# Norm vectors and q's and k's first weight blocks loaded from ScalarE's queue, x^T's first two blocks at the head of SP's

## The chip, the cores and the metric

The kernel runs on one core of one Trainium2 chip. The metric is device time in microseconds (us): the median of three runs before the change is 1878.91 us (1877.92 to 1880.84). All data is float32. Engines: PE is TensorE (matmuls; its weight loads are shown as PEld), ACT is ScalarE, DVE is VectorE, POOL is GpSimd, SP is SyncE, which here only issues transfers.

## What is computed

One encoder layer on 512 tokens of width 2048. Only its beginning matters here: the norm, the projection by w_in, and of that the columns of head 0's q and k.

```python
h = rms_norm(x, pre_mix_g[l])
z = h @ w_in[l]                       # (512 x 2048) @ (2048 x 4096)
q = z[..., :ATTN_WIDTH]; k = z[..., ATTN_WIDTH:2 * ATTN_WIDTH]   # 8 heads of 128
v, u = ...
a = chunked_attention(q, k, v, rel_bias[l])
p = multiscale_pool(u, pool_w[l], pool_scale[l])
x = x + rms_norm(concat(a, p) @ w_o[l], post_mix_g[l])
# then a gated feed-forward of width 5632 with a causal depthwise convolution
```

## The kernel before

**Precision.** A float32 product is made of three matmuls of a reduced format: each operand is split into a high part (ACT rounds it: lines 143 and 146) and a low part (DVE takes what is left: lines 144 and 147), and `mm3` (lines 159 to 161) multiplies high by high, then with one low part, then with the other. Line 146 and 147 also multiply by the norm's gain, which is a column of the tile `vec`. The token's own norm factor is applied later, so the first products need only x^T, the gains and the weights.

**The first loop.** The inner dimension of 2048 is cut into 16 blocks of 128 rows, kb = 0 to 15. For each kb the kernel loads block kb of x^T (128 x 512, 256 KB, into the tiles `xT0` to `xT3`, four blocks in each), splits it into `hT`, and adds 2 x 3 matmuls of 512 columns, three for q and three for k of head 0, to two accumulators. q's and k's weights come in pieces of 1, 3, 4, 4 and 4 blocks (`chunks`), each piece one transfer for q and one for k: 64 KB each for kb = 0, 192 KB each for kb = 1 to 3, 256 KB each for four blocks. Their rows are 128 elements, that is 512 bytes; a row of x^T is 2 KB.

**What sets the order.** PE's order is the order of the program. On the other engines a scheduler orders the instructions at build time; SP keeps the loop's order of transfers. In it SP issues `vec` (line 122, 28 KB), then block 0 of x^T (line 266), q's and k's first pieces (line 271), block 1 of x^T, q's and k's pieces for kb = 1 to 3, then blocks 2, 3 and 4 of x^T, the pieces for kb = 4 to 7, and so on. ACT and DVE take the splits about in this order and each split waits for its own transfer. Transfers signal on eight semaphores in turn, so that from the ninth on the issuing queue waits until the transfer eight places earlier has landed.

**Before the first product.** ACT loads its table (line 130) and does a small activation. PE does nine matmuls of zeros (line 136, 18 passes) from 1.09 us on, while the first transfers are under way.

**Behind the loop.** The loop is followed by v's products and the rest of the layer. v's weights, and all others, come through rings of buffers that are loaded ahead on SP's and POOL's queues.

Of the kernel before, what the change touches and what calls it, by code (L numbers as in the profile page):

```python
# [15 lines left out]
P = 128  # L16
# [7 lines left out]
ATTN = HEADS * DH  # L24
# [19 lines left out]
V_CONV = V_PSCALE + 8  # L44
# [7 lines left out]
def rows(w, r0, c0, a, b):  # L52

    return w[r0:r0 + a * P, c0:c0 + b].rearrange("(a p) c -> p a c", p=P)
# [23 lines left out]
def encoder_layer(ctx: ExitStack, tc: tile.TileContext, x, xT, vecs, rel, post_mix, post_ffn,  # L78
# [7 lines left out]
    nc = tc.nc  # L86
# [18 lines left out]
    def bank(name, at=None):  # L105
        if at is None:
            at = cycle.pop(0)
            cycle.append(at)
        pool = psum if at < 2 else upper_pool
        return pool.tile([P, 512], F32, tag=f"ps{at}", bufs=1, name=name)  # L110

    def acc8(name, which, dt=F32):
        return acc.tile([P, 2048], dt, tag="acc" + which, bufs=2, name=name)

    def raw4(name):
        return big.tile([P, 1024], F32, tag="raw", bufs=6, name=name)

    def w4(name):
        return big.tile([P, 1024], F32R, tag="w4", bufs=8, name=name)

    vec = const.tile([P, V_ALL], F32, name="vec")
    nc.sync.dma_start(vec[:, :V_CONV], vecs[:, :V_CONV])
    ident = const.tile([P, P], F32, name="ident")
    make_identity(nc, ident)
    ones = const.tile([P, 1], F32, name="ones")
# [12 lines left out]
    def col(v, i):  # L138
        return vec[:, v + i:v + i + 1]

    def split(hi, lo, src, scale=None):
        if scale is None:
            rounded = nc.scalar.activation(hi, src, AF.Copy)  # L143
            split.low = nc.vector.tensor_sub(lo, src, f32(hi)).ins  # L144
        else:
            rounded = nc.scalar.activation(hi, src, AF.Copy, scale=scale)
            nc.vector.scalar_tensor_tensor(lo, src, scale, f32(hi), op0=ALU.mult, op1=ALU.subtract)
        split.last = rounded.ins
        return rounded.ins
# [8 lines left out]
    def mm3(ps, l, r, first, last):  # L158
        nc.tensor.matmul(ps, l[0], r[0], start=first, stop=False)  # L159
        nc.tensor.matmul(ps, l[0], r[1], start=False, stop=False)  # L160
        nc.tensor.matmul(ps, l[1], r[0], start=False, stop=last)  # L161
# [4 lines left out]
    def hT4(name, shape):  # L166
        return whole(name).rearrange("p (s a b) -> p s a b", s=2, a=shape)
# [4 lines left out]
    def blk(hT, kb, sl=slice(None)):  # L172
        return tuple(hT[kb // 4][:, part, kb % 4, sl] for part in range(2))
# [20 lines left out]
    def halves(name, w, c0, a, b):  # L194
        n = KD // a
        return [(f"{name}_{i}", rows(w, i * a * P, c0, a, b), a, b) for i in range(n)]

    def head_cols(what, h):
        return {"q": 0, "k": ATTN, "u": 3 * ATTN}[what] + h * P

    def qk_specs(h):
        return halves(f"q{h}", w_in, head_cols("q", h), 8, P), halves(f"k{h}", w_in, head_cols("k", h), 8, P)
# [8 lines left out]
    for h in range(1, HEADS):  # L211
        q, k = qk_specs(h)
# [14 lines left out]
    for n in WO_ORDER:  # L227
        for cc in range(2):
            s = [(f"wo{n}{cc}_{q}", rows(wo_factor[n], q * 256, cc * S, 2, S), 2, S) for q in range(4)]
# [24 lines left out]
    R = const.tile([P, S], F32, name="R")  # L254
    rt = const.tile([P, NT], F32, name="rt")
    const.tile([P, 40], F32, name="place")
    xt = [acc8(f"xT{i}", "AABB"[i]).rearrange("p (a b) -> p a b", a=4) for i in range(4)]
    hT = [hT4(f"hT{i}", 4) for i in range(4)]
    first = {}
    for s in [s for pair in zip(*qk_specs(0)) for s in pair]:  # L260
        first[s[0]] = raw4(s[0] + "r"), w4(s[0] + "h"), w4(s[0] + "l")
    ps0 = {what: bank(what + "0") for what in "qk"}
    chunks = {0: 1, 1: 3, 4: 4, 8: 4, 12: 4}
    for kb in range(KD):
        i, o = divmod(kb, 8)
        nc.sync.dma_start(xt[kb // 4][:, kb % 4, :], xT[kb * P:(kb + 1) * P, :])
        for what in "qk":
            if kb in chunks:
                raw, hi, lo = first[f"{what}0_{i}"]
                sl = slice(o * P, (o + chunks[kb]) * P)  # L270
                nc.sync.dma_start(raw[:, sl].rearrange("p (a b) -> p a b", b=P),
                                  rows(w_in, kb * P, head_cols(what, 0), chunks[kb], P))
                split(hi[:, sl], lo[:, sl], raw[:, sl])
        last_split = split(*blk(hT, kb), xt[kb // 4][:, kb % 4, :], col(V_PREMIX, kb))
        for what in "qk":
            _, hi, lo = first[f"{what}0_{i}"]
            sl = slice(o * P, (o + 1) * P)
            mm3(ps0[what], (hi[:, sl], lo[:, sl]), blk(hT, kb), kb == 0, kb == KD - 1)
# [464 lines left out]
    def hold_rows(tag, name):  # L743
        return [hold(tag, f"{name}{i}", F32).rearrange("p a b -> p (a b)") for i in range(2)]
# [252 lines left out]
    with tc.tile_pool(name="p2", bufs=1, reuse_waits="tile") as p2:  # L997
# [51 lines left out]
        def load_x(t):  # L1049
            xs = hold_rows("wl", f"x{t}")  # L1050
            for j in range(2):
                nc.sync.dma_start(xs[j], x[(2 * t + j) * P:(2 * t + j + 1) * P, :])
            return xs
# [539 lines left out]
```

## Time and profile before

| | |
|---|---|
| median of three runs | 1878.91 us (1877.92 to 1880.84) |
| profiled execution: time, span | 1880.33 us, 1878.6 us |
| outside the span | 1.73 us |
| PE busy | 1859.6 us, 99% of the span |
| DVE, ACT, POOL busy | 80%, 51%, 16% |
| chain that ended last | PE 95%, DVE 2%, ACT 1%, DMA 1%, issue 1% |
| PE idle in the first 50 us | 3.05 us of 50 |
| mean granted clock of PE | 0.997 |

The span runs from the first to the last instruction; the execution's own time is 1.73 us longer. Busy time of PE includes the matmuls of zeros at the start. The granted clock is given as a share of full speed (2.4 GHz); 0.5 is 1.2 GHz. An "xcount" in a row of a timeline or a window counts instructions.

### The profile page before, as it was taken

The page shows a single profiled execution, that of the slowest core. Times are in us where ns is not written, and L with a number is a line of the kernel's source. Part 1 is how long each engine was busy: PE and PEld are TensorE (multiplying, and loading weights), DVE is VectorE, ACT ScalarE, POOL GpSimd, SP SyncE. Part 2 cuts the span into 40 slices and gives each one's busy share as a digit, 9 for nine tenths or more (in the row PEclk, how much of TensorE's full clock was granted, in tenths as well). Part 3 has the DMA queues.
Part 4 walks back from the last instruction along what each step waited for, and adds up shares of the span by engine and source line. Part 5 has one row for each costly group of instructions (what it writes and reads, how often), then busy time and mean ns, then how long its engine had stood idle before and what let it go on. Part 6 is the DMA issues. An engine that isn't in the chain of part 4 may idle for free.

```text
span 1878.6 us, 25181 instructions
## 1 busy us (share of the span) xinstructions
PE 1859.6 (99%) x9674; PEld 1596.4 (85%) x9674; DVE 1499.5 (80%) x1824; ACT 953.6 (51%) x1172; POOL 296.0 (16%) x387
## 2 busy tenths in 40 slices
PE   9999999999999999999999999999999899999998
PEld 7888888888889988888888888888888788888886
DVE  5445445587588989888888888888889899999877
ACT  6333233346488555555455554555545655565543
POOL 4101000000001111221221111111110112222221
PEclk9999999999999999999999999999999999999999
DMA  9747856676877778797977767667677799999997
GB/s 334 214 112 169 228 148 171 166 186 216 286 284 213 213 192 213 187 213 184 230 184 189 183 157 192 165 179 184 156 176 247 223 277 251 252 239 233 222 227 238
DMA packets 177913, 391.41 MB, mean 208 GB/s; under 512 B 11264, under 2 KB 62848, under 8 KB 174720
## 3 DMA queue, kind: packets, MB, share of 16 engines
q1 hardware_dynamic: 130720, 250.32, 40.4%
q0 software_dynamic: 47072, 139.48, 38.5%
q8 instruction: 76, 1.25, 0.3%
q14 instruction: 45, 0.37, 0.1%
HBM read 333.13 MB, written 98.57 MB: 230 GB/s over the span
## 4 chain that ended last, share of the span: by engine, by line
PE 95%; DVE 2%; ACT 1%; DMA 1%; issue 1%; SPq 0%; POOL 0%; POOLq 0%; DVEq 0%; ACTq 0%
PE q L978 27%; PE q L984 14%; PE p L160 6%; PE p L161 6%; PE p L159 6%; PE q L160 3%; PE q L161 3%; PE q L159 3%; PE m L160 2%; PE m L161 2%; PE m L159 2%; PE u L159 2%; PE v L159 2%; PE u L160 2%; PE v L161 2%; PE u L161 2%
## 5 line engine op out<-in xcount | busy, mean ns | idle before, releaser
L978 PE MATMUL q<-gT,wfh 128*128 128x512 f32 x1264 | 329.5, 392 | 0.0
L978 PEld LDWEIGHTS q<-gT,wfh 128*128 128x128 f32 x1264 | 233.1, 189 | 40.6
L978 PE MATMUL q<-h,wfh 128*128 128x512 f32 x960 | 253.7, 392 | 0.1
L143 ACT ACTIVATE wfh<-wx 128x1024 fp32r<-128x1024 f32 x167 | 174.9, 1059 | 131.8 <-PE q L984 72.5
L144 DVE TENSOR_TENSOR wfl<-wx,wfh 128x1024 fp32r<-128x1024 f32 x167 | 202.2, 1221 | 37.3 <-ACT wfh L143 37.2
L160 PE MATMUL p<-bl,ah 128*128 128x512 f32 x544 | 212.6, 391 | 1.8 <-DVE bl L144 1.8
L159 PE MATMUL p<-bh,ah 128*128 128x512 f32 x544 | 212.3, 390 | 1.9 <-ACT bh L143 1.6
L161 PE MATMUL p<-bh,al 128*128 128x512 f32 x544 | 212.3, 390 | 1.8 <-DVE al L144 1.8
L978 PEld LDWEIGHTS q<-h,wfh 128*128 128x128 f32 x960 | 178.3, 189 | 31.1 <-issue 0.4
L984 PEld LDWEIGHTS q<-gT,wfl 128*128 128x128 f32 x1264 | 172.4, 190 | 12.3
L984 PE MATMUL q<-gT,wfl 128*128 128x256 f32 x1264 | 176.2, 282 | 0.0
L143 ACT ACTIVATE bh<-b 128x2048 fp32r<-128x2048 f32 x68 | 129.8, 1917 | 86.7 <-DVE b L687 65.7
L144 DVE TENSOR_TENSOR bl<-b,bh 128x2048 fp32r<-128x2048 f32 x68 | 154.7, 2287 | 10.9 <-PE p L160 6.0
L815 POOL DMA_DIRECT2D wx<-in_w_up x86 | 75.8, 882 | 539.7 <-DVE wfl L144 430.9
L984 PEld LDWEIGHTS q<-h,wfl 128*128 128x128 f32 x960 | 131.0, 190 | 9.4
L984 PE MATMUL q<-h,wfl 128*128 128x256 f32 x960 | 133.9, 282 | 0.0
L143 ACT ACTIVATE wfh<-wy 128x1024 fp32r<-128x1024 f32 x82 | 87.1, 1062 | 86.3 <-PE q L984 81.5
L159 PEld LDWEIGHTS p<-bh,ah 128*128 128x128 f32 x544 | 102.5, 188 | 24.2 <-ACT bh L143 2.0
L160 PEld LDWEIGHTS p<-bl,ah 128*128 128x128 f32 x544 | 102.5, 188 | 23.4 <-DVE bl L144 2.1
L161 PEld LDWEIGHTS p<-bh,al 128*128 128x128 f32 x544 | 102.5, 188 | 23.3 <-DVE al L144 2.2
L730 POOL DMA_DIRECT2D sum<-part x60 | 72.0, 1238 | 256.5 <-DVE part L721 112.9
L144 DVE TENSOR_TENSOR wfl<-wy,wfh 128x1024 fp32r<-128x1024 f32 x82 | 99.8, 1217 | 2.3 <-ACT wfh L143 2.3
(454 smaller groups left out, 3823.6 us busy)
## 6 DMA issues: line engine op xcount, KB each, us to landing
wx<-in_w_up POOLq DMA_DIRECT2D x86, 512.0 KB, 8.0
b<-in_w_down SPq DMA_DIRECT2D x39, 1024.0 KB, 9.0
sum<-part POOLq DMA_DIRECT2D x70, 512.0 KB, 9.3
wx<-in_w_up SPq DMA_DIRECT2D x45, 512.0 KB, 3.6
wy<-in_w_up SPq DMA_DIRECT2D x44, 512.0 KB, 4.6
wz<-in_w_up SPq DMA_DIRECT2D x44, 512.0 KB, 6.1
wy<-in_w_up POOLq DMA_DIRECT2D x39, 512.0 KB, 6.7
wo_sum<-in_w_o POOLq DMA_DIRECT2D x16, 1024.0 KB, 12.0
```

What stands on the lines that cost most here:

```text
L143: rounded = nc.scalar.activation(hi, src, AF.Copy)
L144: split.low = nc.vector.tensor_sub(lo, src, f32(hi)).ins
L159: nc.tensor.matmul(ps, l[0], r[0], start=first, stop=False)
L160: nc.tensor.matmul(ps, l[0], r[1], start=False, stop=False)
L161: nc.tensor.matmul(ps, l[1], r[0], start=False, stop=last)
L730: nc.gpsimd.dma_start(dest, v, accum_op=ALU.add)
L815: self.last_add = nc.gpsimd.dma_start(self.raw[k, what], self.block(k, m, kh), accum_op=ALU.add).ins
L978: nc.tensor.matmul(ps.rearrange("p (a b) -> p a b", a=2), w[0][:, kb], both(h_f[i], kb), start=kb == 0, stop=kb == 7)
L984: nc.tensor.matmul(ps[:, :T], w[1][:, kb], at(h_f[i], kb)[0], start=False, stop=False)
```

## The change

`vec` and the two 64 KB pieces of q and k for kb = 0 are issued on ScalarE's queue instead of SP's. SP's queue begins with blocks 0 and 1 of x^T and then the 192 KB pieces for kb = 1 to 3; from block 2 of x^T on its order is the old one. The transfers of kb = 0 and 1 are issued ahead of the other setup (identity, constants, zeros for PE), the tiles for them are made there, and the loop leaves out what has been issued. No transfer changes its size, and no arithmetic changes.

```diff
-    nc.sync.dma_start(vec[:, :V_CONV], vecs[:, :V_CONV])
+    nc.scalar.dma_start(vec[:, :V_CONV], vecs[:, :V_CONV])
+    xt = [acc8(f"xT{i}", "AABB"[i]).rearrange("p (a b) -> p a b", a=4) for i in range(4)]
+
+    def load_x(kb):
+        nc.sync.dma_start(xt[kb // 4][:, kb % 4, :], xT[kb * P:(kb + 1) * P, :])
+
+    first = {}
+    for n in range(2):
+        for what in "qk":
+            first[f"{what}0_{n}"] = raw4(f"{what}0_{n}r"), w4(f"{what}0_{n}h"), w4(f"{what}0_{n}l")
+
+    def load_first(queue, what, kb, n):
+        queue.dma_start(first[f"{what}0_{kb // 8}"][0][:, kb % 8 * P:(kb % 8 + n) * P].rearrange("p (a b) -> p a b", b=P),
+                        w_in[kb * P:(kb + n) * P, (0 if what == "q" else ATTN):(0 if what == "q" else ATTN) + P].rearrange(
+                            "(a p) b -> p a b", p=P))
+
+    for what in "qk":
+        load_first(nc.scalar, what, 0, 1)
+    for kb in range(2):
+        load_x(kb)
+    for what in "qk":
+        load_first(nc.sync, what, 1, 3)
...
     for kb in range(KD):
         i, o = divmod(kb, 8)
-        nc.sync.dma_start(xt[kb // 4][:, kb % 4, :], xT[kb * P:(kb + 1) * P, :])
+        if kb > 1:
+            load_x(kb)
         for what in "qk":
             if kb in chunks:
                 raw, hi, lo = first[f"{what}0_{i}"]
                 sl = slice(o * P, (o + chunks[kb]) * P)
-                nc.sync.dma_start(raw[:, sl].rearrange("p (a b) -> p a b", b=P),
-                                  rows(w_in, kb * P, head_cols(what, 0), chunks[kb], P))
+                if kb > 1:
+                    load_first(nc.sync, what, kb, chunks[kb])
                 split(hi[:, sl], lo[:, sl], raw[:, sl])
```

SP's queue from the start of the program, before the change (names are tiles with a number behind them; xT0 holds blocks 0 to 3 of x^T, q0_0r and k0_0r the weights of kb = 0 to 7; DMAHW0 to 7 are the eight semaphores):

```order
L122 DMA vec_74<-in_vecs 128x56
L266 DMA xT0_106<-in_xT 128x512
L271 DMA q0_0r_114<-in_w_in 128x128
L271 DMA k0_0r_117<-in_w_in 128x128
L266 DMA xT0_106<-in_xT 128x512
L271 DMA q0_0r_114<-in_w_in 128x3x128
L271 DMA k0_0r_117<-in_w_in 128x3x128
L266 DMA xT0_106<-in_xT 128x512
L266 DMA xT0_106<-in_xT 128x512 [waits DMAHW0_49]
L266 DMA xT1_107<-in_xT 128x512 [waits DMAHW1_49]
L271 DMA q0_0r_114<-in_w_in 128x4x128 [waits DMAHW2_49]
```

SP's queue from the start, now (lines 126 and 134 are the two new helpers):

```order
L126 DMA xT0_76<-in_xT 128x512 x2
L134 DMA q0_0r_80<-in_w_in 128x3x128
L134 DMA k0_0r_83<-in_w_in 128x3x128
L126 DMA xT0_76<-in_xT 128x512
L126 DMA xT0_76<-in_xT 128x512 [waits DMAHW0_49]
L126 DMA xT1_77<-in_xT 128x512 [waits DMAHW1_49]
L134 DMA q0_0r_80<-in_w_in 128x4x128 [waits DMAHW2_49]
```

Block 2 of x^T, the third of line 126's, stands behind four transfers where it stood behind seven.

ACT from the start of the program, before the change (line 146 splits a block of x^T, line 143 a piece of weights):

```order
L130 ACT_TABLE_LOAD
L130 ACTIVATE table_85<-ones_81 128x1 [waits DVE_49]
L146 ACTIVATE hT0_110<-xT0_106,vec_74 128x512 [waits DMAHW1_49,DMAHW0_49]
L143 ACTIVATE q0_0h_115<-q0_0r_114 128x128 [waits DMAHW2_49]
L143 ACTIVATE k0_0h_118<-k0_0r_117 128x128 [waits DMAHW3_49]
L146 ACTIVATE hT0_110<-xT0_106,vec_74 128x512 [waits DMAHW4_49]
L143 ACTIVATE q0_0h_115<-q0_0r_114 128x384 [waits DMAHW5_49]
L143 ACTIVATE k0_0h_118<-k0_0r_117 128x384 [waits DMAHW6_49]
L146 ACTIVATE hT0_110<-xT0_106,vec_74 128x512 [waits DMAHW7_49]
```

ACT from the start, now (lines 167 and 164 are the old 146 and 143):

```order
L122 DMA vec_74<-in_vecs 128x56
L134 DMA q0_0r_80<-in_w_in 128x128
L134 DMA k0_0r_83<-in_w_in 128x128
L151 ACT_TABLE_LOAD
L151 ACTIVATE table_107<-ones_103 128x1 [waits DVE_49]
L164 ACTIVATE q0_0h_81<-q0_0r_80 128x128 [waits DMAHW2_49]
L167 ACTIVATE hT0_128<-xT0_76,vec_74 128x512 [waits DMAHW1_49,DMAHW0_49]
L164 ACTIVATE k0_0h_84<-k0_0r_83 128x128 [waits DMAHW4_49]
L164 ACTIVATE q0_0h_81<-q0_0r_80 128x384 [waits DMAHW5_49]
L167 ACTIVATE hT0_128<-xT0_76,vec_74 128x512 [waits DMAHW3_49]
L164 ACTIVATE k0_0h_84<-k0_0r_83 128x384 [waits DMAHW6_49]
L167 ACTIVATE hT0_128<-xT0_76,vec_74 128x512 [waits DMAHW7_49]
```

Three transfers stand ahead of the table load, and q's pieces for kb = 0 and for kb = 1 to 3 are now split ahead of block 0 and block 1 of x^T. DVE's order follows ACT's. PE's order is unchanged; further on, one pair of ACT's instructions (a square of x^T and the split of a piece of v's weights) changes places.

## Rows read from the trace of the kernel before

**Rows 1.** The page, part 1: busy us, share of the span, instructions.
```profile
PE 1859.6 (99%) x9674; PEld 1596.4 (85%) x9674; DVE 1499.5 (80%) x1824; ACT 953.6 (51%) x1172; POOL 296.0 (16%) x387
```

**Rows 2.** Waits of PE, whole run: us in total, times, longest.
```profile
PE q L159 <- ACT hT L146: 1.4, 1, 1.4
...
PE q L160 <- DVE hT L147: 0.3, 1, 0.3
```

**Rows 3.** Timeline of PE, first 16 us: start, us, operation [idle before it <- releaser].
```profile
1.09 4.21 PE L136 MATMUL idle<-early 128*128 128x128 f32 x18 [1.09 <-DVE early L128]
4.95 0.66 PE L159 MATMUL q<-hT,q_0h 128*128 128x512 f32 x1
...
8.99 0.50 PE L161 MATMUL k<-hT,k_0l 128*128 128x512 f32 x1
10.94 0.50 PE L159 MATMUL q<-hT,q_0h 128*128 128x512 f32 x1 [1.44 <-ACT hT L146]
11.72 0.50 PE L160 MATMUL q<-hT,q_0h 128*128 128x512 f32 x1 [0.28 <-DVE hT L147]
```

**Rows 4.** Windows: stretch, length; busy us of PE, PEld, DVE, ACT, POOL; PEclk, DMA, GB/s.
```profile
9.50:10.94 1.44, 0.00 (x1) 0.01 (x1) 0.02 (x1) 0.78 (x2) 0.00 (x0) 1.00 1.14 357
...
12.06:15.71 3.65, 3.65 (x11) 2.83 (x10) 3.57 (x7) 3.44 (x7) 0.00 (x0) 0.53 1.09 381
15.71:20.00 4.29, 4.29 (x20) 3.57 (x19) 4.25 (x8) 4.16 (x7) 0.00 (x0) 1.00 1.09 385
...
50.00:300.00 250.00, 250.00 (x1182) 210.15 (x1181) 119.80 (x216) 84.02 (x149) 16.65 (x41) 1.00 0.67 171
```

**Rows 5.** Timeline of ACT, first 25 us.
```profile
0.74 1.28 ACT L130 ACT_TABLE_LOAD   x1 [0.74 <-PEq L1582]
2.04 0.20 ACT L130 ACTIVATE table<-ones 128x1 f32<-128x1 f32 x1
3.91 0.72 ACT L146 ACTIVATE hT<-xT,vec 128x512 fp32r<-128x512 f32 x1 [1.67 <-DMA xT<-in_xT]
4.54 0.29 ACT L143 ACTIVATE q_0h<-q_0r 128x128 fp32r<-128x128 f32 x1
...
6.58 0.51 ACT L143 ACTIVATE q_0h<-q_0r 128x384 fp32r<-128x384 f32 x1
7.82 0.52 ACT L143 ACTIVATE k_0h<-k_0r 128x384 fp32r<-128x384 f32 x1 [0.74 <-DMA k_0r<-in_w_in]
10.16 1.98 ACT L146 ACTIVATE hT<-xT,vec 128x512 fp32r<-128x512 f32 x3 [1.82 <-DMA xT<-in_xT]
```

**Rows 6.** Timeline of SP's queue, first 25 us: start, us of issuing, transfer.
```profile
0.74 0.39 SPq L122 DMA_DIRECT2D vec<-in_vecs  x1
...
4.09 1.44 SPq L266 DMA_DIRECT2D xT<-in_xT  x3
```

**Rows 7.** DMA issues at 0.74, 3.56 and 4.09 us: KB each, us from issue to landing.
```profile
vec<-in_vecs SPq DMA_DIRECT2D x1, 28.0 KB, 1.9
...
k_0r<-in_w_in SPq DMA_DIRECT2D x1, 192.0 KB, 4.2
...
xT<-in_xT SPq DMA_DIRECT2D x1, 256.0 KB, 6.0
```

**Rows 8.** Windows of 1 us, columns as in Rows 4.
```profile
2.00:3.00 1.00, 1.00 (x7) 1.00 (x7) 0.00 (x0) 0.23 (x2) 0.47 (x15) 1.00 0.79 205
...
4.00:5.00 1.00, 1.00 (x8) 1.00 (x6) 0.33 (x1) 0.83 (x2) 0.00 (x0) 1.00 0.63 199
...
7.00:8.00 1.00, 0.86 (x3) 0.39 (x3) 0.93 (x2) 0.26 (x2) 0.00 (x0) 1.00 0.73 184
...
9.00:10.00 1.00, 0.49 (x2) 0.17 (x1) 0.00 (x0) 0.00 (x0) 0.00 (x0) 1.00 1.04 361
```

**Rows 9.** The page, part 5, POOL's issues: busy us, mean ns of one, idle before.
```profile
L815 POOL DMA_DIRECT2D wx<-in_w_up x86 | 75.8, 882 | 539.7 <-DVE wfl L144 430.9
...
L730 POOL DMA_DIRECT2D sum<-part x60 | 72.0, 1238 | 256.5 <-DVE part L721 112.9
```

More of the change, by code (lines that the diff above doesn't have):

```diff
@@ L256, in encoder_layer @@
     const.tile([P, 40], F32, name="place")
-    xt = [acc8(f"xT{i}", "AABB"[i]).rearrange("p (a b) -> p a b", a=4) for i in range(4)]
     hT = [hT4(f"hT{i}", 4) for i in range(4)]
-    first = {}
-    for s in [s for pair in zip(*qk_specs(0)) for s in pair]:
-        first[s[0]] = raw4(s[0] + "r"), w4(s[0] + "h"), w4(s[0] + "l")
     ps0 = {what: bank(what + "0") for what in "qk"}
```

## The prediction, made before the changed kernel ran

> **What bounds the kernel now.** I read the engines' shares first, then PE's waits, then the first 20 us engine by engine, since the change touches nothing else. PE is busy for 99% of the span [rows 1], so a change can gain only what PE loses, and it must lie where PE waits. Of PE's waits the loop that the change touches has two worth naming, 1.4 us and 0.3 us [rows 2]. Both stand at the same place: the last matmul of kb = 1 starts at 8.99 and ends at 9.49, the first of kb = 2 starts at 10.94, the second, which needs the low part of the same block, at 11.72 [rows 3]. The reader is to follow this back: ACT splits block 2 of x^T from 10.16, after 1.82 us without work, and is released by a transfer [rows 5]; that transfer was issued at 4.09 [rows 6] and took 6.0 us to land [rows 7], that is until 10.1. So **the landing of block 2 of x^T** sets when PE goes on, and from there on it is not stopped again in this loop: it is busy for 4.29 of 4.29 us at 15.71 to 20, and for 250 of 250 at 50 to 300 [rows 4].
>
> The gap has a second price. PE's granted clock is 1.00 in the gap, and from 12.06 to 15.71 its mean is 0.53, so nearly all of that at the lower of the two levels (1.2 GHz, against 2.4) [rows 4]. Over 3.65 us that is 0.47 x 3.65 = 1.7 us of lost matmul time. Everything that a change to this start could give back is thus some 1.4 + 0.3 + 1.7 = 3.4 us, under 0.2% of the time (3.8 us), about what a measurement of this kernel can tell from no change. That bounds the whole matter before any detail, but for a start of PE ahead of 4.95, which the zeros of line 136 exclude: they run from 1.09 to 5.30, and the first real matmul overlaps their end [rows 3].
>
> **Part 1, SP's queue is shorter.** Before block 2 of x^T SP issues seven transfers, from 0.74 to 4.09 [rows 6], so 3.35 / 7 = 0.48 us each. Now it issues four: block 2 goes out at 0.74 + 4 x 0.48 = 2.66, 1.43 us earlier. The semaphores that the next ones wait for are those of the vectors, block 0 of x^T and so on; the vectors landed 1.9 us after their issue [rows 7], that is by 2.7 if issued at 0.74 on ACT, so SP isn't held at block 3.
>
> How much of the 1.43 us reaches the landing depends on what filled the 6.0 us. The vectors needed 1.9 us with little else in flight, the 192 KB for k 4.2, block 2 of x^T 6.0 [rows 7]: the longer the queue, the later the landing, so a good part of it is waiting in the 16 DMA engines, and the same bytes stand ahead of block 2 after the change as before. If the engines had been full all the time, the landing would move by nothing; if never, by 1.43. They had pauses: their share was 0.79 in 2 to 3 us, 0.63 in 4 to 5 and 0.73 in 7 to 8, against 1.04 in 9 to 10, when transfers stood in line [rows 8]. Taken against 1.04 these three slices hold 0.25 + 0.41 + 0.31 = 0.97 us of pause ahead of block 2's landing, and an issue that is 1.43 us ahead can fill them. I take **1.0 us**, with 0 and 1.43 as bounds; it lies nearest to the rows of the engines' share, since they count the thing itself. The landing comes at 9.1, and the first matmul of kb = 2 at 10.94 - 1.0 = 9.9.
>
> **Part 2, ACT issues three transfers first.** No row shows a transfer issued by ACT. The nearest are SP's, 0.39 us (0.48 with the step to the next) [rows 6], and POOL's, 0.88 to 1.24 us [rows 9]. I take SP's 0.48, because both issue the same kind of load here and POOL's is another queue. ACT's table load then starts at 0.74 + 3 x 0.48 = 2.2, ends with its small activation 1.28 + 0.20 later, at 3.7, and the splits of q's piece (0.29) and of block 0 (0.72) end at 4.7 [rows 5], ahead of 4.95. Before, ACT stood idle for 1.67 us there [rows 5]; that idle time hides the issues. Cost nothing. At POOL's dearest price the table activation ends at 0.74 + 3.72 + 1.48 = 5.9 and the first real matmul would be near 7.0, two us late; but ACT would still have done kb = 1's splits (k's small piece 0.29 like q's, then 0.51, 0.72 and 0.52 [rows 5]: 2.0 us) by 9.0, before block 2 lands. PE would then finish kb = 1 about 10.3 instead of 9.9, which takes 0.4 us off the gain. So this part costs 0 to 0.4 us, and I take 0. Who waits behind the issues is the table load and all of ACT's splits; the cover is the gap before kb = 2.
>
> **Part 3, the new order on ACT and DVE.** Block 1 of x^T is now split behind q's 192 KB piece. Before, that piece was split at 6.58, in 0.51 us and with no idle time ahead of it [rows 5], so it had landed by then; if it lands no sooner now, block 1's split (0.72) runs from 7.1 to 7.8, just when k's piece is split in the trace, and kb = 1 ends as before, at 9.5. With the piece issued 1.43 us earlier it ends earlier. Either way kb = 2's block decides. Cost 0. q's and k's first pieces on their own queue share the engines with blocks 0 and 1; kb = 0 has its slack from the zeros, and all these bytes stand ahead of block 2 anyhow.
>
> **Part 4, the gap and the clock.** kb = 1's last matmuls wait for k's 192 KB piece, which ACT splits at 7.82 when it lands [rows 5]; this is issued 1.43 us earlier too and stands in the same line, so PE ends kb = 1 about 1 us earlier as well, at 8.5. The gap stays about 1.4 us, and after such a gap the clock fell in the trace. So I let the clock fall again for as long: no difference.
>
> **The sum.** 1.0 us of gain, 0 of cost: 1880.33 - 1.0 = 1879.3 for an execution like the profiled one (1878.6 span and 1.73 around it, which nothing here changes). The profiled execution lay 1.42 us above the median of the runs, so the median becomes 1878.91 - 1.0 = **1877.9 us**. The bounds of the terms alone (0 to 1.43, less up to 0.4) give 1877.5 to 1879.3.
>
> **Rivals.**
> *The clock holds (B).* If PE's gap becomes shorter, or falls at another moment, the clock may stay at 2.4 GHz, and 1.7 us more come back: 1878.91 - 2.7 = 1876.2. For it: the clock was still at 1.00 through the gap itself and fell only about when PE was back at full work [rows 4], so where the low stretch lies isn't fixed by the gap alone. Against it: the gap is likely to stay as long as it is. With the full 1.43 us and no gap at all it would be 3.4 us, or 1875.5.
>
> *The engines were the bound (D).* If the pauses in the share come from the 512-byte rows of the weights and not from late issues, no transfer lands sooner and the time stays at 1878.9. For it: in 7 to 8 us the share was 0.73 although block 2 had been issued three us before [rows 6, 8]; that pause wasn't SP's. Leaving that slice out, the gain of part 1 is 0.66 us, inside my range. The same result comes if a later stage, bound by its loads, takes the gain back. The Trainium skill (DMA: Bandwidth & Descriptors, section "Issuing engines are not separate DMA queues") speaks against the change here: transfers from several issuing engines share the same 16 DMA engines, and a second issuer saves only issue time, usually small beside the transfer. By that rule alone D would be the result.
>
> *The line gets deeper (C), slower.* Blocks 2, 3 and 4 of x^T were split without a break, 1.98 us for three [rows 5], so blocks 3 and 4 had landed nearly with block 2: the engines work on several transfers at once. Now q's and k's 256 KB for kb = 4 to 7 are also issued earlier, and if they are served among block 2's packets, each takes 256 KB at 357 GB/s [rows 4] = 0.73 us. With both, 1.46 - 1.0 = 0.5 us slower: 1879.4. It decides when more than 1.0 / 0.73 = 1.4 such transfers come in ahead that didn't before. Against it: they wait for the landing of earlier ones, and one queue serves in order.
>
> **How the numbers follow.** My forecast (A, 1877.9) 0.45; B 0.20; D 0.20; C 0.15. The range has to hold A to D: B's 1876.2 and C's 1879.4, each with about 0.9 us for the spread of a median whose three runs lay 2.9 us apart: 1875.2 to 1880.3. Faster by over 0.2% (below 1875.15) needs B, the full 1.43 us and a favourable draw: 0.06. Slower by over 0.2% (above 1882.7) isn't reached by any case; C with a dear issue on ACT, a second fall of the clock and an unfavourable draw: 0.04. Within 0.2%: 0.90.
>
> **What would show it.** In the new profile block 2 of x^T is issued near 2.7 and ACT splits it near 9.1; the first matmul of kb = 2 stands near 9.9, that of kb = 0 still near 4.9; ACT's three issues take 1.4 us in all and its table load starts near 2.2; the clock has one low stretch of some 3.6 us. I am wrong if block 2 still lands at 10.1 (D) or later (C), if the low stretch is gone (B) or comes twice, or if ACT's issues take 1 us each and the first product starts at 6 or later.

## The result

The changed kernel takes **1889.06 us** (median of five runs, 1888.38 to 1890.05) against 1878.91 (five runs, 1877.56 to 1880.84): ratio 1.0057, 95% interval 1.0046 to 1.0068. It is slower by 10 us, where 1.0 us of gain was forecast and the range ended at 1880.3. The profiled execution took 1889.9 us, its span is 1888.1.

The start of the program, on which the prediction spent all its working, is faster in this profile than in the profile before. The loss is 1.45 ms later.

### The profile page after: what moved, and what is told of

It is laid out like the page before. It is cut to its first block, busy times and chain, and to the rows that moved or that the text cites. A ratio compares the mean times of both kernels' runs of the same rounds, so it can differ in the third digit from the quotient of the medians.

```text
span 1888.1 us, 25181 instructions
## 1 busy us (share of the span) xinstructions
PE 1859.9 (99%) x9674; PEld 1597.7 (85%) x9674; DVE 1499.5 (79%) x1824; ACT 952.6 (50%) x1172; POOL 296.0 (16%) x387
## 4 chain that ended last, share of the span: by engine, by line
PE 96%; DVE 2%; DMA 1%; ACT 1%; issue 0%; POOL 0%; SPq 0%; POOLq 0%; ACTq 0%; DVEq 0%
PE q L996 27%; PE q L1002 14%; PE p L180 7%; PE p L182 7%; PE p L181 7%; PE q L181 3%; PE q L180 3%; PE q L182 3%; PE m L181 2%; PE m L182 2%; PE m L180 2%; PE k L180 2%; PE k L182 2%; PE k L181 2%; PE u L180 2%; PE v L180 2%
## 5 line engine op out<-in xcount | busy, mean ns | idle before, releaser
L180 PE MATMUL p<-bh,ah 128*128 128x512 f32 x544 | 213.0, 392 | 13.4 <-ACT bh L164 13.4
```

## The profile after

Waits of PE over the whole run, after the change (as [rows 2]: us in total, times, longest; the lines have moved, 180 to 182 are the old 159 to 161, 164 the old 143):

```profile
PE p L180 <- ACT bh L164: 13.4, 1, 13.4
PE p L181 <- DVE bl L165: 1.5, 1, 1.5
...
PE q L180 <- ACT hT L167: 0.7, 1, 0.7
```

The 1.4 us of [rows 2], ahead of kb = 2, is gone; at the start there is now a wait of 0.7 us ahead of kb = 0. And one single wait of 13.4 us stands in another stage: `p` are the products of the last stage (the feed-forward's output with w_down), `bh` the high part of a piece of w_down.

The start, timeline of PE (as [rows 3]):

```profile
1.09 4.21 PE L157 MATMUL idle<-early 128*128 128x128 f32 x18 [1.09 <-DVE early L149]
6.03 0.80 PE L180 MATMUL q<-hT,q_0h 128*128 128x512 f32 x1 [0.72 <-ACT hT L167]
...
11.21 0.39 PE L180 MATMUL q<-hT,q_0h 128*128 128x512 f32 x1
...
13.93 0.39 PE L180 MATMUL q<-hT,q_0h 128*128 128x512 f32 x1
```

These are the first products of kb = 0, 2 and 4. kb = 0 starts 1.1 us later than in [rows 3], kb = 2 with no pause ahead of it, and kb = 4 at 13.93, where the kernel before has it at 15.94: 2.0 us are won by then. The timeline of ACT and SP's queue show why kb = 0 is late and kb = 2 isn't (as [rows 5] and [rows 6]):

```profile
0.74 0.41 ACTq L122 DMA_DIRECT2D vec<-in_vecs  x1
...
1.17 0.46 ACTq L134 DMA_DIRECT2D q_0r<-in_w_in  x1
...
2.15 1.28 ACT L151 ACT_TABLE_LOAD   x1 [2.15 <-issue]
2.66 2.12 SPq L126 DMA_DIRECT2D xT<-in_xT  x3
...
5.05 0.31 ACT L164 ACTIVATE q_0h<-q_0r 128x128 fp32r<-128x128 f32 x1 [1.41 <-DMA q_0r<-in_w_in]
...
7.52 1.93 ACT L167 ACTIVATE hT<-xT,vec 128x512 fp32r<-128x512 f32 x3
```

Landing times of these transfers (as [rows 7]: KB, us from issue to landing):

```profile
vec<-in_vecs ACTq DMA_DIRECT2D x1, 28.0 KB, 3.2
...
q_0r<-in_w_in ACTq DMA_DIRECT2D x1, 64.0 KB, 3.9
...
xT<-in_xT SPq DMA_DIRECT2D x1, 256.0 KB, 4.3
```

Block 2 of x^T is issued at 2.66 and lands 4.3 us later, at 7.0 instead of 10.1; ACT takes it up without waiting. q's first piece, issued at 1.17, needs 3.9 us and lands at about 5.05, and ACT, which splits it ahead of block 0, waits 1.41 us for it.

**Where the 13.4 us are.** SP's queue around 1440 us, first before the change, then after (start, us of issuing with the waits inside a group, transfer; `gc` are two halves of the gated product read back from HBM, `b` pieces and sums of w_down):

```profile
1434.31 3.70 SPq L623 DMA_DIRECT2D b<-in_w_down  x2
1438.45 0.92 SPq L623 DMA_DIRECT2D gc<-gd  x2
1439.42 3.80 SPq L623 DMA_DIRECT2D b<-wd_sum  x3
```

```profile
1432.29 3.71 SPq L641 DMA_DIRECT2D b<-in_w_down  x2
1436.11 21.10 SPq L641 DMA_DIRECT2D gc<-gd  x2
1457.26 2.58 SPq L641 DMA_DIRECT2D b<-wd_sum  x3
```

PE gets here 2.0 us earlier, and so does SP. But the two loads of gc take 21.10 us to go out instead of 0.92: the second is held. The wait table of SP's queue in 1430 to 1480 us of the changed kernel names the releaser. The second line is that of the same table of the kernel before, where PE holds SP for 2.4 us only:

```profile
SPq L641 <- PE p L182: 20.1, 1, 20.1
...
SPq L623 <- PE p L161: 2.4, 1, 2.4
```

SP waits for PE, and PE then waits for SP. The chain that ended last, after the change (start, us, what):

```profile
1457.26 0.68 SPq L641
1457.94 0.04 issue
1457.99 10.52 DMA b<-wd_sum
1468.51 0.02 issue
1468.53 1.92 ACT bh L164
```

and PE's first product behind it, after the change and before:

```profile
1470.49 0.80 PE L180 MATMUL p<-bh,ah 128*128 128x512 f32 x1 [13.42 <-ACT bh L164]
...
1460.64 0.49 PE L159 MATMUL p<-bh,ah 128*128 128x512 f32 x1 [1.57 <-ACT bh L143]
```

The second half of gc goes out at 1456.9, when PE comes to the end of the products it has (the last of them ends at 1457.07). Behind it go the three loads of `b`, which had gone out by 1443.2 before; then 10.52 us for the transfer, 1.92 for the split, and PE resumes. Before the change the same pause was 1.57 us (1459.07 to 1460.64). So PE comes 2.0 us earlier, loses 13.42 - 1.57 = 11.85 us and resumes 9.85 us late. The span is 9.5 us longer, since all that follows takes 0.35 us less: the later waits of this stage are shorter by 1.3 us (1.5 and 1.1 instead of 1.8, 1.8 and 0.3), and most of that is lost again behind the longer pause, where the products start 0.43 us apart up to 1478.10 (granted clock 0.50, the lower level, from 1470.49 to 1475); before the change they did so only up to 1466.12.

**Why the load of gc waits for PE.** The order of instructions on SP is the same there in both kernels. Its waits are not. Before:

```text
L623 DMA gc0_13133<-gd0_0_3583 128x2048 [waits DMAHW6_49,PE_49]
L623 DMA gc1_13135<-gd0_1_3584 128x2048 [waits DMAHW7_49,DMASW3_49]
L623 DMA b7_13138<-wd_sum7_3611 128x2048 [waits PE_49]
```

After:

```text
L641 DMA gc0_13133<-gd0_0_3583 128x2048 [waits DMAHW6_49,DMASW1_49]
L641 DMA gc1_13135<-gd0_1_3584 128x2048 [waits DMASW3_49,DMAHW7_49,DVE_49,PE_49]
L641 DMA b7_13138<-wd_sum7_3611 128x2048
```

`gc1` now waits for PE, `gc0` no longer. Here a load waits for PE when its buffer lies where an operand lay that PE still reads. So the places have moved, and the diff shows by what: it makes q's and k's first tiles (`raw4`, `w4`) at the top of the program, ahead of `hT`. All three kinds live in one pool, `big`, which lays its kinds out in the order in which they are first asked for. From the code's sizes, in KB per partition: before hT 0 to 64, raw 64 to 88, split weights 88 to 120; after raw 0 to 24, split weights 24 to 56, hT 56 to 120. The last stage lays its buffers over the freed pool from the bottom, `wh` at 0 to 16, then gc's two of 8 KB at 16 to 32. Before, both fell on an hT tile; now the second falls on two split weight tiles, one of which at that time holds the high part of a left factor of the stage's first products. No row of a profile prints an address, but the addresses in the two built programs agree with these places, and the count of PE's instructions that `gc1` waits for (7872) is that of the last product that reads this left factor. The same programs show one thing more: `b5`, the load after `b7`, waits for PE in both, but now for a later product (count 7873 instead of 7801); it lies on the low part of the same left factor. The experiments test whether the places make the loss.

## The experiments

The theory (P, place): the loss comes from the order in which tiles are first allocated, not from the loads. The first rival (T): the earlier transfers, or the semaphores in which they take turns, make the wait. Within the start three more things were open: what the issue time is worth, what the clock costs, and whether all three transfers had to move.

### Places put back, loads as changed

```diff
+    hT = [big.tile([P, 8 * S], F32R, tag="hT", bufs=4, name=f"hT{i}").rearrange("p (s a b) -> p s a b", s=2, a=4)
+          for i in range(4)]
     first = {}
...
-    hT = [hT4(f"hT{i}", 4) for i in range(4)]
```

> The changed kernel, but the four hT tiles are allocated ahead of q's and k's weight tiles in their common pool, as in the kernel before; the loads are those of the change. Theory P (place): the 13.4 us wait of PE in the last stage comes from where the tiles lie: the weight tiles, now made first, push hT to another place, and a later tile that reuses it must wait for PE. Then the wait is back at about 1.6 us, the second load of gd is issued within 1 us of the first instead of 20 us later, and the 2.0 us gained by kb = 4 remain: 1876.9 us. Rival T (timing): the wait comes from transfers that now run at other times, or from the semaphores they share; then it stays at 13.4 us and the time at 1889.

Measured: 1877.41 us (11 runs, 1875.76 to 1878.82), ratio 0.9993 (0.9984 to 1.0002) to the kernel before, whose median in these runs is 1878.42. SP's two loads of gc and PE's wait:

```profile
1434.33 1.19 SPq L642 DMA_DIRECT2D gc<-gd  x2
```

```profile
PE p L182 <- ACT bh L166: 1.5, 1, 1.5
```

T has fallen: the loads of the change are all there, and the wait is 1.5 us. In this profile the first product of kb = 4 comes at 11.93, sooner than in that of the change:

```profile
11.93 0.39 PE L182 MATMUL q<-hT,q_0h 128*128 128x512 f32 x1
```

### Places alone, loads as before

```diff
-    hT = [hT4(f"hT{i}", 4) for i in range(4)]
     first = {}
     for s in [s for pair in zip(*qk_specs(0)) for s in pair]:
         first[s[0]] = raw4(s[0] + "r"), w4(s[0] + "h"), w4(s[0] + "l")
+    hT = [hT4(f"hT{i}", 4) for i in range(4)]
```

> The kernel before with one edit: q's and k's first weight tiles are allocated ahead of the hT tiles, all loads as before. Theory P (place): the start is unchanged (first product of kb = 4 at 15.9 us), the wait in the last stage is 13.4 us instead of 1.6, and the time is 1878.9 + 11.5 = 1890.4 us. Rival T (timing): the loads of the start are what makes the wait, so this kernel keeps 1878.9.

Measured: 1889.7 us (five runs, 1888.94 to 1890.34), ratio 1.0059 (1.0047 to 1.0072). One moved line; the built program differs from the one before in nothing but places and the waits of eleven instructions of the last stage. The whole loss is there:

```profile
1435.87 20.78 SPq L623 DMA_DIRECT2D gc<-gd  x2
```

```profile
PE p L159 <- ACT bh L143: 13.6, 1, 13.6
```

The start came out otherwise than expected: kb = 4 at 13.28, not at 15.9, with the same loads.

### The change as it is, the last stage's buffers in another order

```diff
-        for r in (later["wh"], half_g, raw2, later["raw1"], product_part, later["wl"], slot_h, slot_l, scratch):
+        for r in (half_g, later["raw1"], product_part, scratch, later["wh"], raw2, later["wl"], slot_h, slot_l):
```

> The changed kernel as it is, loads and early places included; only the order in which the last stage's buffers are laid out is another, so that the two buffers for gd (gc) come to lie on q's and k's old raw weight tiles instead of on split weight tiles that PE reads to the end of its first products. Theory P (place): the load of gc's second half no longer waits for PE, the 13.4 us wait shrinks to about 2 us, and the time is 1877 to 1879. Rival (the early places do harm by something else than this wait): the wait moves but the time stays above 1885.

Measured: 1876.59 us (11 runs, 1875.92 to 1878.18), ratio 0.9991 (0.9982 to 1.0). gc's buffers now begin at 0 and by the sizes above lie on raw tiles; the wait is gone with the early allocation still as in the change:

```profile
1436.16 1.10 SPq L641 DMA_DIRECT2D gc<-gd  x2
```

```profile
PE p L180 <- ACT bh L164: 1.1, 1, 1.1
```

So it isn't the early order itself that harms, but which old tiles the loads of this stage lie on. One load of `b` still waits for PE here, 7.5 us, but for an earlier product, and PE doesn't lose by it:

```profile
SPq L641 <- PE p L182: 7.5, 1, 7.5
```

### The held load behind the three others

```diff
-            (a11, a12), (a21, a22), s = load(0), load(1), scratch("s")
-            v, state = {1: a11, 2: a12, 3: a12, 5: s, 7: a21, 6: s, 4: a22}, None
+            (a11, a12) = load(0)
+            if c:
+                a21, a22 = load(1)
+            s, state = scratch("s"), None
             if c < 2:
                 i = yield
+            if not c:
+                a21, a22 = load(1)
+            v = {1: a11, 2: a12, 3: a12, 5: s, 7: a21, 6: s, 4: a22}
```

> The changed kernel with the places as in the change, but SP issues the load of gc's second half behind the loads of the three factors b7, b5 and b6 instead of ahead of them. Theory Q (most of the wait is the queue: the three loads stand behind the waiting one): they go out near 1440 us, gc's second half still at about 1457, its data reach PE by way of a subtraction and a split some 8.5 us later, and PE's wait is about 8.5 us instead of 13.4. Rival: the three loads wait for PE by themselves as well, they go out at 1457 too, and the wait stays at 13 us or grows.

Measured: 1887.78 us (one run). The rival of this run is right, and Q has fallen:

```profile
1434.27 0.44 SPq L641 DMA_DIRECT2D gc<-gd  x1
1435.12 21.21 SPq L641 DMA_DIRECT2D b<-wd_sum  x3
1456.43 0.41 SPq L641 DMA_DIRECT2D gc<-gd  x1
```

```profile
PE p L180 <- ACT ah L164: 17.2, 1, 17.2
```

The loads of `b` are held by PE as well: their buffers too lie on tiles that PE still reads. PE's wait grows to 17.2 us, since gc, which needs a subtraction and a split more, now comes last. So this move in the queue doesn't help while the places are wrong. (That the time is a little below that of the change doesn't speak against this: the two later waits of 1.5 and 1.1 us are gone here, and kb = 4 came at 12.06 instead of 13.93.)

### Block 2 of x^T held back

```diff
     for what in "qk":
         load_first(nc.sync, what, 1, 3)
+    nc.sync.dma_start(vec[:1, V_CONV:V_CONV + P], vecs[:1, V_CONV:V_CONV + P])
```

The base is the kernel with the places put back.

> As the first kernel with the places put back, with one transfer of 512 bytes on SP ahead of block 2 of x^T; it waits for the vectors' semaphore turn, so that block 2 is issued at about 4.0 us as before the change instead of 2.7, while all bytes ahead of it are the same. Theory I (issue time sets the landing): block 2 lands at 8.3 to 9.2 us. Rival E (two queues at work, or the same bytes sooner in line, set it): it lands near 7, as with the issue at 2.7.

Measured: 1877.55 us (one run). Block 2 (first of these three) goes out at 3.93 and needs 4.9 us:

```profile
3.93 1.37 SPq L126 DMA_DIRECT2D xT<-in_xT  x3
```

```profile
xT<-in_xT SPq DMA_DIRECT2D x1, 256.0 KB, 4.9
```

It lands at 8.8 instead of 6.9, with the same bytes ahead of it but for the 512. In the five profiles with the issue at 2.65 or 2.66 it lands at 6.9 to 7.2, so 8.8, though a single profile, lies outside their spread. Theory I holds: the landing follows the issue, and 1.27 us of delay at the issue went with 1.9 at the landing. PE lost nothing by it: kb = 0 began at 5.95 here too, and kb = 2 at 10.82 with no pause ahead of it.

### The vectors alone on ScalarE

```diff
-    for what in "qk":
-        load_first(nc.scalar, what, 0, 1)
-    for kb in range(2):
-        load_x(kb)
-    for what in "qk":
-        load_first(nc.sync, what, 1, 3)
+    for kb, n in (0, 1), (1, 3):
+        load_x(kb)
+        for what in "qk":
+            load_first(nc.sync, what, kb, n)
```

The base is again the kernel with the places put back.

> Layout as before the change; only the vectors are issued by ScalarE, and SP begins with block 0 of x^T and keeps the old order. Theory I (issue time sets block 2): block 2 is issued at 3.6 instead of 4.1 and lands about 0.5 us earlier than 10.1, the first product of kb = 0 stays near 4.9, PE's gap and the low clock stay: 1878.4 us. Rival E (the move of q's and k's first pieces isn't needed; the engines gain once SP begins with x^T): block 2 lands near 7 to 8 as in the changed kernel and, with kb = 0 on time, the time is 1875 to 1876.

Measured: 1877.33 us (11 runs, 1876.05 to 1878.25), ratio 0.9992 (0.9983 to 1.0001). Block 2:

```profile
3.60 1.44 SPq L126 DMA_DIRECT2D xT<-in_xT  x3
```

```profile
xT<-in_xT SPq DMA_DIRECT2D x1, 256.0 KB, 4.7
```

It lands at 8.3, and the first product of kb = 0 stays at 4.95. Each theory is half right: block 2 lands earlier than I's 9.6, and PE's pause ahead of kb = 2 and the slow products are gone, as E has it, but the time isn't E's 1875 to 1876. It lies between the two expectations, and can't be told from that of the kernel in which all three transfers moved: with q's and k's first pieces on SP, kb = 0 is on time and block 2 a little later; with them on ScalarE it is the other way round.

### More zeros

```diff
-WARM = 9
+WARM = 12
```

The base is the kernel with the places put back.

> As the first kernel of this set, with 12 matmuls of zeros instead of 9, so that PE works on them until about 6.7 us and has no pause before the first product. Theory C (the clock follows the pause): no low stretch of the clock, kb = 0 starts near 6.7 instead of 6.0, but all its matmuls run at full speed, the first product of kb = 4 comes at about 12.2 us instead of 13.9, and the time is 1875.2 us. Rival: the clock falls all the same, or DVE's splits set the pace; then kb = 4 starts at 13.5 to 14.5 and the time is 1876.5 to 1877.5.

Measured: 1876.79 us (11 runs, 1876.15 to 1878.08), ratio 0.9991 (0.9982 to 0.9999). kb = 0 starts at 6.23 behind the zeros, kb = 4 at 12.13 (first and 25th row of this loop):

```profile
1.09 5.49 PE L159 MATMUL idle<-early 128*128 128x128 f32 x24 [1.09 <-DVE early L151]
6.23 0.77 PE L182 MATMUL q<-hT,q_0h 128*128 128x512 f32 x1
...
12.13 0.39 PE L182 MATMUL q<-hT,q_0h 128*128 128x512 f32 x1
```

The trace is as theory C expects, but the gain isn't shown: the profiled execution of the kernel with 9 zeros had no slow stretch either and reached kb = 4 at 11.93, and the medians of the two, 1876.79 and 1877.41, lie within each other's runs. That the clock follows the pause stays open. The length of the pause alone doesn't decide it: with the same loads ahead of kb = 0, pauses of 0.57, 0.65 and 0.72 us (the runs with other late places and with block 2 held back, and the change) are followed by products 0.43 us apart, pauses of 0.49 and 0.69 us (places put back, held load behind the others) are not.

## Why the prediction was wrong

**The step that failed: "the change touches nothing else".** The prediction read the engines' first 20 us because the edit stands there, and called everything behind unchanged ("1878.6 span and 1.73 around it, which nothing here changes"). Of its rivals only D has a sentence on a later stage, and there that stage takes the gain back at most; none lets a later stage lose. The diff does touch something else: it moves the first allocation of three kinds of tiles that share a pool, and a stage 1.45 ms later lays its buffers over that pool. Places alone give 1889.7, the loads with the places put back 1877.41, and other late places 1876.59; so this is shown, and accounts for the whole loss. What could be seen ahead was the waits of each instruction: the front of this document compares the orders, which are the same on SP from block 2 on; the waits of the loads of gc, b7 and b5 on SP, and of a few instructions on ACT and DVE, are not.

**What the prediction said of the start** can be judged from the kernel with the places put back. Its gain is 1878.42 - 1877.41 = 1.0 us, with an interval from a gain of 3.0 to a loss of 0.4 (0.9984 and 1.0002 of 1878.42), against a forecast of 1.0. That the two agree is luck, for the terms came out otherwise.

- The bound of 3.4 us for all that the start could give back: too small. It counts only PE's two waits and the slow products. In the profile with the places put back kb = 4 comes 4.0 us earlier than in the profile before (11.93 against 15.94), though kb = 0 begins 0.8 us later: the twelve products of kb = 0 and 1, which the bound took for busy time that can't be won, took 3.4 us there and 4.5 before.
- Part 1, block 2's landing: mis-sized. The issue came at 2.66 as worked out, the landing in the profile of the change at 7.0, not 9.1: 3.1 us sooner than in the profile before. The bound of 1.43 was wrong in itself: it let the landing move by no more than the issue, while the time from issue to landing shrank too (4.3 us at an issue at 2.66, 4.7 at 3.60, 4.9 at 3.93, against 6.0 at 4.09). Part of the 3.1 is spread between runs of the same loads: where only the places were moved, block 2, issued at 4.09 as before, landed after 5.0 us and not 6.0. Rivals D and C are out: no run with the loads of the change shows block 2 at 10.1 or later. That SP isn't held at block 3 was wrong, without a cost that shows: the vectors took 3.2 us on ScalarE's queue and not 1.9, and SP waited 0.8 us for them there. The rule of the Trainium skill that was weighed there (DMA: Bandwidth & Descriptors, section "Issuing engines are not separate DMA queues": a second issuer saves only issue time, usually small beside the transfer) agrees with the runs in its first half: with the issue held back to 3.93, block 2 lands at 8.8 beside the second queue, not far from the 9.1 without it. One issue is small here too, 0.48 us beside 1.9 to 6.0 to the landing. But the issues ahead of block 2 add up, and 1.27 us of them went with 1.9 at the landing.
- Part 2, ACT: the issues cost 0.41 to 0.46 us each and the table load began at 2.15, as forecast. That the splits end at 4.7, "ahead of 4.95", failed nevertheless. The prediction gave the landing of q's first piece no term of its own ("kb = 0 has its slack from the zeros", part 3). It took 3.9 us, against 2.4 on SP's queue before, so kb = 0 began at 6.03. This was costed at 0 to 0.4; it took back 1.1 us at kb = 0. The row before:

```profile
q_0r<-in_w_in SPq DMA_DIRECT2D x1, 64.0 KB, 2.4
```

- Part 4, the clock: in the profile of the change kb = 0 and 1 ran at the slow spacing instead of kb = 2 and 3. From 7.41 to 9.97 the products start 0.43 us apart, as at 12.4 to 15 in the kernel before (two rows of each, the change first). Together with part 2 this is why 3.1 us at block 2 became 2.0 at kb = 4. That the clock falls again was right of this profile only; in the one with the places put back it doesn't show, as rival B has it, and yet the median there is not B's 1876.2.

```profile
8.69 0.63 PE L182 MATMUL k<-hT,k_0l 128*128 128x512 f32 x1
9.11 0.63 PE L180 MATMUL q<-hT,q_0h 128*128 128x512 f32 x1
...
13.24 0.63 PE L161 MATMUL k<-hT,k_0l 128*128 128x512 f32 x1
13.67 0.63 PE L159 MATMUL q<-hT,q_0h 128*128 128x512 f32 x1
```

## What to carry to other kernels

An edit that makes a tile earlier can move other tiles: where pools lay out their buffers in the order of first use, and later stages reuse the memory, compare what every instruction waits for, over the whole program and before any timing, and not only the order; for a wait that stands in both, compare the count too. When a kernel gets slower by far more than the edited stretch can lose, look first for one long wait elsewhere, then ask which queue the released instruction stood in. The load that waited here for the engine that needs its data was a place to fix, not a load to move.

## What the runs showed beyond that

- **The clock's row and the spacing can disagree.** The window of the changed kernel's slow stretch (columns as in [rows 4]):

```profile
6.82:10.39 3.57, 3.57 (x9) 2.80 (x9) 3.57 (x7) 3.44 (x7) 0.00 (x0) 1.00 1.08 363
```

  The granted clock reads 1.00, its upper level, yet the products start 0.43 us apart, just as in the stretch of [rows 4] whose mean is 0.53. Two more profiles, with other late places and with block 2 held back, show the same at this point. The spacing is what the time follows; why the row says 1.00 isn't settled.
- **The same loads give starts that differ by 2.7 us.** With only the places moved, the loads of the kernel before had kb = 4's first product at 13.28 and no slow stretch, against 15.94 in the profile before:

```profile
13.28 0.39 PE L159 MATMUL q<-hT,q_0h 128*128 128x512 f32 x1
```

  The 27 runs of the kernel before span 3.5 us (1877.13 to 1880.67); one profile of such a start is one draw, and the 3.4 us that the prediction saw to be had there were those of a slow one.
- **Small transfers landed later from the second queue.** The 28 KB of vectors took 3.0 to 3.2 us on ScalarE's queue in seven profiles, with a block of x^T issued on SP's at the same moment, and 1.8 and 1.9 at the head of SP's in two [rows 7]. Whether the second queue or the company of x^T makes the difference no run shows.
